# A hybrid GLA and differential-attention layer: a fourth paired projection, branch sums on GpSimd, and an attention whose order of matmuls is a table

## The chip, the cores and the metric

The kernel runs on one core of a Trainium2 chip. The metric is the device time of one execution in microseconds; the time of a kernel is the median of its runs. TensorE is called PE (its weight loads PEld), VectorE DVE, ScalarE ACT, GpSimd POOL; DMAs are issued by SyncE (SP).

## The reference

One layer over 1024 latent tokens x and 256 context tokens, width 1024, all in float32. Cut to what matters here:

```python
pl = project(modulate(x, sh_x, sc_x), w_in)      # 1024 -> 9248 columns, split into:
#  gq 512, gk 512, gv 1024, gate 1024, low rank 32, dq 1024, dk 1024, dv 1024, dgate 1024, m_gla 1024, m_diff 1024
pc = project(modulate(ctx, sh_c, sc_c), w_in)
la = log_sigmoid(lr @ w_dec + b_dec) / 16        # per direction: the decay
o_gla  = bidir_gla(q, k, v, la_f, la_b, s_f, s_b)        # 4 heads, chunks of 64, both directions
a = softmax(q1 k1^T / 8) - lam * softmax(q2 k2^T / 8)    # 8 heads, keys: context + latent = 1280
o_diff = a @ dv
a = merge_heads(rms_norm(o_gla) * gla_gain) * silu(gla_gate)
b = merge_heads(rms_norm(o_diff) * diff_gain * (1 - lam_init)) * silu(diff_gate)
y = sigmoid(m_gla) * (a @ w_br_gla) + sigmoid(m_diff) * (b @ w_br_diff)
out = x + g_x * (y @ w_out)
```

## The kernel before

**Precision.** A float32 operand is split into a rounded part hi and a remainder lo (`split`: a copy on ACT, a subtraction on DVE), and a product is three matmuls (`mm3`: hi hi, hi lo, lo hi) into one PSUM bank. A projection of 1024 inputs onto a tile of 128 x 512 is thus 8 k-blocks x 3 = 24 matmuls.

**The planner.** The program is written as coroutines. `Driver` runs them against a model of the engines' times and so decides, when the kernel is built, in which order instructions stand in each engine's queue. A coroutine waits by yielding an event, a time, or a slot of a tag (`acq`; `rel` gives it back). Lower `prio` goes first. On the chip every engine takes its queue in order. `TAGS` lists the buffers by tag with their pool and count; pools are opened and closed stage by stage.

**Stages.** (1) The prologue: modulation, norm, transposes into `h0`, `h1`, `hc`. (2) `stream` in `phase_a`: projections `gk`, `gq` and the first half of the GLA gate, `gg[0]`, as direct jobs; beside them `job_lr`, `job_la` (the decay), `job_gate` (the ada gate for `w_out`, in `raw` buffers) and `sums` (the block sums s1 to s4 of the layer's input, stored to `d_s`). (3) `pairs`: the projections of `BY7`, which are `gv`, `dv`, `dg`, each by a scheme with seven block products instead of eight. `pair_weights` loads and combines their weights, `loads` brings the sums back into `g5` buffers once `ev_la` and the stored sums are there; `presums` builds, in windows set by `WIN`, the block sums of `w_out`. (4) `to_gla` opens the GLA's buffers; `gla_head` runs four heads in a chain while `stream` goes on with the late jobs as filler: `dk` (two halves), `gg[1]`, `dq` (two halves), and the first half of the mix gates (`post_m`). (5) The attention (`att_scores`, `att_tr`, `att_av`, `att_fin`): for each of 8 heads and 8 query tiles ("score tiles", 64 in all) scores of two components (S), maxima on DVE, exponentials on ACT, the mix of both on DVE, transposes on PE (T), a split into hi and lo (ACT and POOL), and for two query tiles together the product with V (A). `fill` runs beside it with the lowest priority: the rest of the mix gates and the product a @ `w_br_gla`, in half-tiles of 24 matmuls, of which number i is let go when score tile `PACE` x i = 1.3 i has been issued. The planner chooses between S, T, A and fill by priority and readiness. (6) When all scores are done `to_c` opens the last buffers; `prepare` loads the operands of b @ `w_br_diff`, builds their block sums (`OPS`) on DVE and splits them (`SPLITS`); `diff` multiplies seven block products. (7) `right`, `left` and `stream` in `phase_c` do the same for `w_out`, add x and store.

Of the kernel before, what the change touches and what calls it, by code (L numbers as in the profile page):

```python
# [20 lines left out]
P = 128  # L21
# [211 lines left out]
class Hybrid:  # L233
# [18 lines left out]
        ya=("sbC", 8), yb=("sbC", 8), yc=("sbC", 8), yf=("sbC", 8), yg=("sbC", 8), sf=("sbC", 2), o=("sbC", 4), wr=("sbC", 8),  # L252
# [5 lines left out]
                 sbA1="right", sbA2="right", sbW="right", sbB2="right",  # L258
                 psA="left", psW="left", psB="left", psC="left", psA1="right", psB1="right", psD="right")

    def __init__(self, tc, nc, a, out):
        self.tc, self.nc, self.a, self.out = tc, nc, a, out
        self.n = 0
# [17 lines left out]
    def t(self, tag, shape, dt=F32):  # L281
        self.n += 1
        pool, bufs = self.TAGS[tag]
# [92 lines left out]
    def build(self):  # L376
        tc = self.tc
        with (
# [4 lines left out]
            with tc.manual_schedule(engines={ENG.PE, ENG.Activation, ENG.DVE, ENG.Pool}):  # L383
# [8 lines left out]
                self.close("psC", "psW", "psD", "sbW", "sbC", "sb", "sbE")  # L392

    def scratch(self):
# [15 lines left out]
        self.ev_gbt = Event()  # L410
        self.d_y = [d(f"d_y{i}", [P, S]) for i in range(8)]
# [32 lines left out]
    def consts_late(self):  # L444
# [34 lines left out]
        yield from self.rope_tables(1)  # L479
# [271 lines left out]
    def job_gate(self):  # L751
# [5 lines left out]
        for n in range(2):  # L757
            o = 2048 + n * 512
            for kk in range(NK // 2):
                yield from self.acq("raw")  # L760
                raw = self.t("raw", [P, 2, 512])
# [10 lines left out]
                self.rel("raw", e)  # L772
# [22 lines left out]
    def job_tr(self, wd, n, halves, post):  # L795
# [9 lines left out]
        items = [(s, half) for half in halves for s in range(4)]  # L805
# [13 lines left out]
    def phase_a(self):  # L819
# [5 lines left out]
        self.ev_plr, self.ev_lr, self.ev_la, self.ev_gb = [Event() for _ in range(4)]  # L825
# [15 lines left out]
        def tra(c0, halves, post):  # L841
            return c0, lambda wd, n: self.job_tr(wd, n, halves, post)
# [21 lines left out]
        def stream():  # L864
# [4 lines left out]
            for n, j in enumerate(late):  # L869
                if n == 3:  # L870
                    d.spawn(self.rope_tables(0), prio=2)
                yield from j[1](wd2, n)
# [9 lines left out]
        d.spawn(self.job_gate(), At(110.0), prio=2)  # L882
# [11 lines left out]
    BY7 = (("gv", C_GV), ("dv", C_DV), ("dg", C_DG))  # L894

    def sums(self):
# [5 lines left out]
        for k in range(4):  # L902
# [3 lines left out]
            yield from self.acq("g5", 2)  # L906
            x, y = (self.t("g5", [P, 2, 640]) for _ in range(2))
# [1761 lines left out]
```

## Time and profile before

| what | value |
|---|---|
| median of 3 runs | 1625.38 us (1624.56 to 1626.67) |
| the profiled execution's own time | 1624.13 us |
| its span, first to last instruction | 1622.0 us |
| granted PE clock | 1.00 throughout |
| PE instructions | 8277 matmuls |
| HBM | 206.33 MB read, 100.14 MB written |

An engine's busy time is the union of its instructions; the ends of matmuls are modelled, and a matmul of 512 columns is shown as about 389 ns long although the next one starts sooner, so counts in a stretch of time say more of PE's rate than busy times. Lines such as L339 and L201 are helpers through which all matmuls and all ACT, DVE and POOL operations pass; groups are told apart by their tiles, written out<-in.

### The profile page before, as it was taken

Reading aid. Unit: us, or ns where it says so; the run is one execution under the profiler, and the core shown is the slowest. Engines: PE = TensorE matmul, PEld = TensorE weight load, DVE = VectorE, ACT = ScalarE, POOL = GpSimd, SP = SyncE. Lnnn points to the kernel's source line nnn. Section 1 sums busy time; section 2 is a strip of 40 time slices with the busy share of each in tenths; the row PEclk is TensorE's granted clock in tenths of the full one; section 3 lists DMA queues with packets and bytes.
Section 4 is the critical chain, followed back from the end, with each engine's and each line's share of the span. In section 5 each row is a group of like instructions: output and inputs, shape, how many; then the busy total and the mean of one; then the engine's idle time right before and its main releaser. Section 6 shows DMA issues by size and latency. Waiting matters only on the chain.

```text
span 1622.0 us, 24267 instructions
## 1 busy us (share of the span) xinstructions
PE 1601.3 (99%) x8277; PEld 1335.4 (82%) x8277; DVE 1210.8 (75%) x2095; ACT 821.4 (51%) x1689; POOL 596.6 (37%) x647
## 2 busy tenths in 40 slices
PE   8999999999999999999999999999999999999999
PEld 3688888888888888888888788888888888888887
DVE  4788874556678798677772798888888878649994
ACT  4766532244433545564352666666666655535431
POOL 1510200000156566454640446555555556610000
PEclk9999999999999999999999999999999999999999
DMA  8567879688784585655358145443457753354662
GB/s 308 182 214 263 292 241 338 264 309 309 243 271 143 179 256 155 199 156 163 118 163 237 59 124 143 114 121 100 122 134 217 233 143 104 91 191 175 201 220 104
DMA packets 248730, 308.06 MB, mean 190 GB/s; under 512 B 21496, under 2 KB 161696, under 8 KB 248608
## 3 DMA queue, kind: packets, MB, share of 16 engines
q1 hardware_dynamic: 248608, 306.53, 59.7%
q8 instruction: 65, 1.06, 0.3%
q14 instruction: 57, 0.47, 0.1%
HBM read 206.33 MB, written 100.14 MB: 189 GB/s over the span
## 4 chain that ended last, share of the span: by engine, by line
PE 88%; DVE 6%; DMA 2%; ACT 2%; issue 2%; POOL 0%; SPq 0%; DVEq 0%; ACTq 0%
PE mm L339 33%; PE mb L339 10%; PE s L339 8%; PE b L339 7%; PE mc L339 6%; PE tp L339 5%; PE b L365 4%; PE go L339 4%; PE gt L339 4%; PE gs L339 4%; PE tp L365 2%; DVE sm L201 2%; PE mz L339 1%; DVE h L201 1%; ACT e L201 1%
## 5 line engine op out<-in xcount | busy, mean ns | idle before, releaser
L339 PE MATMUL mm<-w,h 128*128 128x512 f32 x1260 | 317.5, 401 | 0.0
L339 PEld LDWEIGHTS mm<-w,h 128*128 128x128 f32 x1260 | 231.6, 188 | 45.9 <-issue 0.5
L201 DVE TENSOR_REDUCE sm<-s 128x1 f32<-128x1024 f32 (+1 forms) x192 | 193.4, 1040 | 43.6 <-PE s L339 41.9
L339 PE MATMUL mb<-h,wt 128*128 128x512 f32 x816 | 220.9, 405 | 1.3 <-DVE ft L201 1.3
L201 ACT ACTIVATE e<-s,sm 128x1280 f32<-128x1280 f32 x128 | 170.1, 1330 | 88.4 <-DVE sm L201 70.3
L201 POOL TENSOR_SCALAR at<-ac 128x512 fp32r<-128x512 f32 x128 | 99.8, 780 | 238.7 <-ACT ac L201 222.9
L339 PE MATMUL s<-hk,aq 128*128 128x512 f32 (+1 forms) x768 | 177.2, 363 | 3.4 <-ACT e L201 2.7
L201 POOL TENSOR_TENSOR at<-ac,at 128x512 fp32r<-128x512 f32 x128 | 174.4, 1363 | 10.7
L339 PEld LDWEIGHTS mb<-h,wt 128*128 128x128 f32 x816 | 144.0, 189 | 26.2 <-DVE ft L201 1.5
L339 PE MATMUL mm<-h,w 128*128 128x512 f32 x576 | 137.8, 394 | 2.0 <-ACT p L201 1.1
L339 PEld LDWEIGHTS s<-hk,aq 128*128 128x128 f32 x768 | 122.1, 189 | 20.9 <-ACT e L201 4.2
L339 PE MATMUL b<-at,vv 128*128 128x256 f32 x960 | 130.8, 287 | 0.0
L339 PEld LDWEIGHTS mm<-h,w 128*128 128x128 f32 x576 | 106.8, 188 | 25.1 <-DVE h L201 1.5
L201 DVE TENSOR_TENSOR w<-raw,w 128x512 fp32r<-128x512 f32 x120 | 87.0, 747 | 47.1 <-ACT w L201 45.8
L339 PEld LDWEIGHTS b<-at,vv 128*128 128x128 f32 x960 | 120.3, 190 | 1.3
L201 POOL TENSOR_TENSOR sm<-sm,nhalf 128x2 f32<-128x2 f32 (+2 forms) x94 | 112.5, 1197 | 20.6 <-DVE sm L201 15.3
L201 DVE SCALAR_TENSOR_TENSOR e<-e,sm,e 128x1280 f32<-128x1280 f32 x64 | 117.7, 1839 | 1.5
L201 ACT ACTIVATE ac<-b 128x512 f32<-128x512 f32 x121 | 72.1, 598 | 83.5 <-PE b L365 83.4
L201 ACT ACTIVATE w<-raw 128x512 fp32r<-128x512 f32 x120 | 72.2, 627 | 72.9 <-PE go L339 21.3
L201 POOL TENSOR_TENSOR p<-p,gdif 128x512 f32<-128x512 f32 x12 | 16.8, 1411 | 238.1 <-DVE p L201 216.0
L201 ACT ACTIVATE p<-mm 128x512 f32<-128x512 f32 (+1 forms) x107 | 61.6, 587 | 76.1 <-PE mm L339 72.5
L365 PE MATMUL b<-ident,e 128*128 128x128 f32 x604 | 93.7, 272 | 0.0
(324 smaller groups left out, 3011.8 us busy)
## 6 DMA issues: line engine op xcount, KB each, us to landing
raw<-in_w_in SPq DMA_DIRECT2D x63, 512.0 KB, 4.7
g<-d_s SPq DMA_DIRECT2D x32, 640.0 KB, 6.1
aq<-d_qT SPq DMA_DIRECT2D x128, 128.0 KB, 3.9
d_dv<-pl SPq DMA_DIRECT2D x40, 256.0 KB, 3.6
gv<-d_v SPq DMA_DIRECT2D x40, 256.0 KB, 3.4
d_kT<-pl SPq DMA_DIRECT2D x40, 256.0 KB, 2.6
hk<-d_kT SPq DMA_DIRECT2D x32, 320.0 KB, 5.1
vv<-d_dv SPq DMA_DIRECT2D x16, 640.0 KB, 6.5
```

The costliest lines, as they stand in the source:

```text
L201: self.ins = f(out, *args, **kw).ins
L339: self.ins = self.nc.tensor.matmul(out, lhsT, rhs, start=start, stop=stop, skip_group_check=more).ins
L365: self.nc.tensor.transpose(out, src, self.ident[:n, :n])
```

## The change

It has these parts.

- The GLA gate becomes a fourth entry of `BY7`; its two direct jobs go. In return the late stream gets half a job more of the mix gates (`NM = 2`, `NS = 2` of 4 column blocks), which `fill` no longer does (`fill_from` 6 in place of 4).
- The stages ahead of the pairs: the decay takes the absolute value on ACT and needs one DVE operation less; `job_gate` starts at 70 in place of 110 and uses `x4`; the reload of the sums waits for new events `ev_lg` and `ev_sg`, set when the last parts hold their `g5` buffers, in place of `ev_la`; the first pair's weights use other buffers; the key's rotary table is loaded later; the four blocks of `presums` go one to each pair.
- Attention: `att_order` writes out one order of all S, T and A; each of them waits for its turn (`turn`, `passed`). Scores run `LEAD = 4` tiles ahead. The first queries are loaded into a `raw` buffer before the GLA has ended.
- `presums_a`: w_br_diff's block sums s1 to s4 are made by POOL during the attention and stored to `d_ps`; `prepare` loads them back. The loads of the last branch's other operands begin once the last scores are done, block by block of the attention's output (`ev_bp`), with buffers that lie in those of keys (`yf`), queries and POOL's inputs (`yg`), and exponentials (`sbD`).

```diff
-        wt=("sbW", 4), ft=("sbW", 2), aq=("sbB2", 4), vv=("sbB2", 3),
-        e5=("sbB", 6), at4=("sbB", 6), at2=("sbB", 2), ac=("sbB", 2), b1k=("sbB", 5), fin=(None, 2),
+        wt=("sbW", 4), ft=("sbW", 2), aq=("sbG", 4), xa=("sbG", 4), vv=("sbB", 3),
+        e5=("sbF", 6), at4=("sbB", 6), at2=("sbB", 2), ac=("sbB", 2), b1k=("sbB", 5), fin=(None, 2),
...
-        jobs = [tra(C_GK, [0, 2, 1], self.post_gk), tra(C_GQ, [0, 1], self.post_gq), gg[0]]
-        late = [dk[0], dk[1], gg[1], dq[0], dq[1]]
-        NM = 1
+        jobs = [tra(C_GK, [0, 2, 1], self.post_gk), tra(C_GQ, [0, 1], self.post_gq)]
+        late = [dk[0], dk[1], dq[0], dq[1]]
+        NM = 2
         for m in range(NM):
-            late.insert(5, tra(C_MG + m * 512, [0, 1], lambda s, half, pm, m=m: self.post_m(4 * m + s, half, pm)))
-        self.fill_from = 4 * NM
+            late.insert(2 + 3 * m, tra(C_MG + m * 512, [0, 1], lambda s, half, pm, m=m: self.post_m(4 * m + s, half, pm),
+                                            self.NS if m else 4))
+        self.fill_from = 4 + self.NS
...
-        d.spawn(self.job_gate(), At(110.0), prio=2)
+        d.spawn(self.job_gate(), At(70.0), prio=2)
...
-    BY7 = (("gv", C_GV), ("dv", C_DV), ("dg", C_DG))
+    NR, NS, TG = 3, 2, 60.0
+    BY7 = (("gv", C_GV), ("dv", C_DV), ("dg", C_DG), ("gg", C_GG))
...
+                    if g == 0:
+                        tag = dict(w111="raw", w211="x4", w120="rope", w221="l5", w121="pl").get(f"{n}{kk}", tag)
...
-    WIN = ((0, 1), (2,), (3,))
+    WIN = ((0,), (1,), (2,), (3,))
...
-            yield self.ev_la
+            yield self.ev_lg
+            yield self.ev_sg
...
-            yield self.act.activation(et, pm, AF.Identity, bias=bcol)
+            yield self.act.activation(et, pm, AF.Abs, bias=bcol)
...
-                    yield self.dve.scalar_tensor_tensor(et, mt, 2.0, et, ALU.mult, ALU.subtract)
...
-                    self.act.activation(ex[j], ex[j], AF.Exp)
+                    self.act.activation(ex[j], ex[j], AF.Exp, scale=-1.0)
...
     def att_queries(self):
-        yield self.ev_b2
+        yield self.wlast
...
+                if (hd, pr) == (0, 0):
+                    yield from self.acq("raw")
+                    early = self.t("raw", [P, 2, 2, 256], F32R)
+                elif (hd, pr) == (0, 1):
+                    yield self.ev_b2
...
     def att_values(self):
-        yield self.ev_q[0, 0]
+        yield self.ev_sb
...
+    LEAD, AHEAD0 = 4, 3
+    def att_order(self):
+        S = lambda u: [("S", u, 0), ("S", u, 1)]
+        T = lambda u: [("T", u, g) for g in range(3)]
+        A = lambda p: [("A", p, 0), ("A", p, 1)]
+        order = sum((S(u) for u in range(self.AHEAD0)), [])
+        for o in range(-1, 65, 2):
+            t, a, s = T(o + 1), A((o - 1) // 2), S(o + self.LEAD + 1)
+            order += T(o) + S(o + self.LEAD) + [t[0], a[0], t[1], a[1], s[0], t[2], s[1]]
+        top = dict(S=64, T=64, A=32)
+        order = [x for n, x in enumerate(order) if 0 <= x[1] < top[x[0]] and x not in order[:n]]
+        self.turns, self.ev_turn = order, {x: Event() for x in order}
+        self.d.set(self.ev_turn[order[0]])
...
+                    yield from self.turn("T", 8 * hd + qt, g)
...
+                    self.passed("T", 8 * hd + qt, g)
...
-    ORDER = ("b11", "b12", "b22", "a12", "b21", "a21", "a22")
+    ORDER = ("b11", "b21", "b22", "a12", "s2", "s1", "s3", "a22", "s4")
...
-        OPS = (("S1", "a21", "a21", "a22", add, ("l_a21", "l_a22"), 2), ("S2", "a11", "a21", "a11", sub, ("S1", "a11"), 2),
-               ("S4", "a12", "a12", "a11", sub, ("S2", "a12"), 4), ("S3", "a11", "a22", "a11", sub, ("S4", "s2"), 4),
-               ("T3", "b12", "b22", "b12", sub, ("l_b12", "l_b22"), 2), ("T2", "b11", "b12", "b11", add, ("T3", "b11"), 2),
+        OPS = (("T3", "b12", "b22", "b12", sub, ("l_b12", "l_b22"), 2), ("T2", "b11", "b12", "b11", add, ("T3", "l_b11"), 2),
...
+    def presums_a(self):
+        d, wb = self.d, self.a["w_br_diff"][0]
+        sub, add = ALU.subtract, ALU.add
+        yield self.ev_sb
+        def op(n, k, o, x, y, f, i):
+            yield self.ev_u[min(63, 2*i+2)]
+            yield d.on("POOL", x, y)
+            self.pool.tensor_tensor(o, x, y, f)
+        for k in range(4):
+            x = {}
+            for r, c in ((1, 0), (1, 1), (0, 0), (0, 1)):
+                yield from self.acq("xa")
+                x[r, c] = self.t("xa", [P, 512])
+                self.dma(x[r, c], wb[c * 512 + k * P:c * 512 + (k + 1) * P, r * 512:(r + 1) * 512])
+            a11, a12, a21, a22 = x[0, 0], x[0, 1], x[1, 0], x[1, 1]
+            ops = (("s1", a21, a21, a22, add), ("s2", a11, a21, a11, sub), ("s4", a12, a12, a11, sub), ("s3", a22, a22, a11, sub))
+            for i, (n, *q) in enumerate(ops):
+                yield from op(n, k, *q, 4 * k + i)
+            for n, o, *_ in ops:
+                self.store([(self.d_ps[n][k], o)], ("xa", 1), ev=self.ev_ps[n, k])
...
-        Z = ("mz", "mz", "mc", "mb")
+        Z = ("mc", "mb", "mz", "mz")
...
+            yield from self.idle("aq", "kk", "xa")
+            Driver.places = tuple(range(512, HK, 512))
+            d.set(self.ev_y0)
+            yield from self.idle("e5")
+            self.close("sbF")
+            self.open("sbD")
+            d.set(self.ev_c1)
             yield self.ev_att
-            yield from self.idle("b1", "e5", "b1k", "aq", "kk", "vv", "at4", "at2", "ac")
-            self.close("psB1", "sbB2", "sbB", "sbK")
+            yield from self.idle("b1", "b1k", "vv", "at4", "at2", "ac")
+            self.close("psB1", "sbB")
```

More of the change, by code (lines that the diff above doesn't have):

```diff
@@ L282, in t @@
         self.n += 1
+        if tag == "yf":
+            self.ny += 1
+            if dt not in self.ys:
+                self.ys[dt] = self.t("hk", [P, HK], dt)
+            x = self.ys[dt][:, (self.ny % 8) * 512:(self.ny % 8 + 1) * 512]
+            self.d.ready[self.d.key(x)] = self.d.now
+            return x
+        if tag == "yg":
+            self.ng += 1
+            tag = ("aq", "xa")[self.ng % 2]
         pool, bufs = self.TAGS[tag]
@@ L804, in post_ @@
             return post(s, half, pm[:, :256 if half == 2 else 512])
-        items = [(s, half) for half in halves for s in range(4)]
+        items = [(s, half) for half in halves for s in range(ns)]
         return self.job(wd, n, items, lambda it, k: [self.ev_h[k, it[1]]],
@@ L977, in free @@
             yield ev_r[g, k]
-            self.rel(slots[g, "w11", k // 2][0], max(e, ev_r[g, k].t), 1 + k // 2)
+            tag = slots[g, "w11", k // 2][0]
+            self.rel(tag, max(e, ev_r[g, k].t), 1 + (tag == "x2"))
         def run():
@@ L2231, in fill @@
             kind = todo[n][0]
-            one = todo[n][:2] in ((1, 6), (1, 7))
+            one = todo[n][:2] in ((1, 6), (1, 7)) or todo[n + 1][0] != kind
             two = [n] if one else [n, n + 1]
@@ L2336, in split @@
             e = yield from self.split(x, *ev[n, k].w)
-            if i > 2 and (src != "a11" or k % 2):
+            if src in ("a11", "e11", "b12"):
+                if k % 2:
+                    self.rel("raw", e)
+            elif i > 2 or src[0] in "as":
                 self.rel(RAW[src], e)
```

151 lines of the change are left out of this document (103 added, 48 removed).

## The prediction

> **What bounds the kernel now.** I read the page's busy times first, then its chain, then the list of what TensorE (PE) waited for.
>
> ```profile
> PE 1601.3 (99%) x8277; PEld 1335.4 (82%) x8277; DVE 1210.8 (75%) x2095; ACT 821.4 (51%) x1689; POOL 596.6 (37%) x647
> ...
> PE 88%; DVE 6%; DMA 2%; ACT 2%; issue 2%; POOL 0%; SPq 0%; DVEq 0%; ACTq 0%
> ```
> ```profile
> engine line waited for: us in total, times, longest us
> PE tp L365 <- DVE p L201: 5.0, 1, 5.0
> PE s L339 <- ACT e L201: 2.7, 3, 1.1
> ```
>
> PE is busy for 1601.3 of 1622.0 us and its longest wait is the 5.0 us before the first transpose, at the start. A busy share can hide gaps between pipelined matmuls, so I cut the span into stages and counted matmuls in them (columns: stretch, length, then busy time and count of PE, PEld, DVE, ACT, POOL, clock, DMA share, GB/s):
>
> ```profile
> 162.00:206.00 44.00, 44.00 (x194) 36.09 (x193) 37.27 (x49) 24.57 (x36) 10.08 (x7) 1.00 0.85 289
> 206.00:302.00 96.00, 96.00 (x426) 79.47 (x425) 57.96 (x88) 29.74 (x51) 3.00 (x2) 1.00 0.87 309
> ...
> 397.50:474.50 77.00, 76.63 (x338) 63.13 (x337) 54.34 (x78) 36.11 (x63) 18.18 (x13) 1.00 0.75 250
> 474.50:887.50 413.00, 412.68 (x2065) 346.40 (x2063) 298.39 (x553) 191.27 (x512) 223.42 (x276) 1.00 0.61 181
> 887.50:1398.00 510.50, 507.25 (x3092) 439.17 (x3093) 424.22 (x784) 317.79 (x642) 283.30 (x264) 1.00 0.47 132
> ```
>
> The first row is the direct job of one half of the GLA gate, the second the paired projection `gv`, the third the paired `dg`, the fourth the GLA beside the late stream, the fifth the attention. In the second row a 512-column matmul costs 96.0/426 = 0.225 us, in the first 44.0/194 = 0.227 us: PE streams without gaps there, at a granted clock of 1.00. So what is taken off PE's count is worth its full price, provided that operands still come in time; and what is only hurried beside PE is worth nothing.
>
> **The gate as a fourth pair.** Before, each half of the gate is 8 tiles x 8 k x 3 = 192 matmuls, and the first half's stage took 44.0 us; the second half costs at least the same in the late stream: 88.0 us together. As a pair it is what `dg` is: 7 products x 4 tiles x 4 k x 3 = 336 matmuls, and that stage took 77.0 us. Saving 88.0 - 77.0 = 11.0 us, on the path. The pair brings the additions on weights and outputs that `dg` has; DVE is at 54.34 of 77.00 us there, so they hide behind PE. If that cover were gone, the stage would last as long as DVE's work: still under 77. Moving one block of presums into each of the four pairs only spreads work that the pairs hide already: 0.
>
> **What must now be ready 44 us earlier.** The first half's direct job stood ahead of the pairs. Without it the first product on the sums s2 comes 44 us sooner:
>
> ```profile
> 234.21 1.98 PE L339 MATMUL mm<-w,g 128*128 128x512 f32 x8
> ```
> ```profile
> 194.03 1.28 SPq L304 DMA_DIRECT2D g<-d_s  x1
> ...
> 205.57 0.32 SPq L304 DMA_DIRECT2D d_s<-g  x1
> ```
> ```profile
> DMA to landing us min/median/max: 2.2/5.2/9.7
> ```
> ```profile
> L201 DVE TENSOR_TENSOR w<-raw,w 128x512 fp32r<-128x512 f32 x120 | 87.0, 747 | 47.1 <-ACT w L201 45.8 <-PE tp L339 0.9 <-PE go L339 0.4
> ...
> L201 DVE SCALAR_TENSOR_TENSOR p<-p,mm 128x512 f32<-128x512 f32 x19 | 12.8, 681 | 1.7 <-ACT p L201 1.5
> ...
> L201 DVE SCALAR_TENSOR_TENSOR g<-g,g 128x1280 f32<-128x1280 f32 x8 | 11.9, 1484 | 0.0
> ```
>
> These are PE's first product on a stored sum, the first reload of a sum and the store of s2's last block, the landing times of these transfers, and DVE groups. The product falls at 234.2 - 44 = 190.2 us; the fourth block of s2 is due 3 x 15 matmuls later, at 190.2 + 45 x 0.225 = 200.3. In this profile that block is stored at 205.6, and with two median transfers of 5.2 us it is back at 216: 16 us late. Against that stands what leaves DVE before it: the eight `g<-g,g` of the decay (11.9 us, which ACT's Abs and the negative scale make needless, at ACT's old cost), the 8 weight splits of the gate's first half (8 x 0.747 = 6.0) and its 8 gate operations (8 x 0.681 = 5.4), 23.3 us in all; the ada gate's sums also start 40 us earlier, in another buffer. DVE is at 37.27 of 44.00 us in this stretch, so most of what leaves it brings the chain forward. The first pair's weights get buffers of their own (`x4`, `rope`, `pl`), so that they don't queue behind `raw`. Bounds 0 and +16 us; I take +1, near the lower end, because 23.3 is more than 16.
>
> **GLA against the late stream.** The late stream loses the gate's second half (44 us) and gains half a job of the mix gate, 4 tiles = 96 matmuls = 22 us, which leaves the attention's fill. On PE's sum that is 0 (bounds -1 and +1). But the stream was what PE did while the GLA's chain ran:
>
> ```profile
> 479.39 0.70 POOL L201 MEMSET fresh<- 128x516 f32 x2
> ```
> ```profile
> 867.49 0.60 PE L365 MATMUL tp<-ident,gp 128*128 128x128 f32 x4
> 867.84 19.34 PE L339 MATMUL mm<-h,w 128*128 128x512 f32 x84
> 887.86 2.60 PE L339 MATMUL s<-hk,aq 128*128 128x512 f32 x12 [0.69 <-ACT p L201]
> ...
> 908.20 1.19 PE L339 MATMUL s<-hk,aq 128*128 128x512 f32 x4 [1.01 <-ACT e L201]
> ...
> 928.62 1.19 PE L339 MATMUL s<-hk,aq 128*128 128x512 f32 x4 [1.09 <-ACT e L201]
> ```
>
> The GLA starts 5 us behind the pairs, and its last transposes end at 868.1, or 393.6 us behind them; the stream ends 413 us behind them, with 19 us of pure stream at the end. Now the stream lasts 413 - 44 + 22 = 391 us. If the GLA keeps its pace, PE runs dry for 393.6 - 391 = 2.6 us: +3. Bounds 0 (the gate's second half also leaves DVE and POOL in this stage) and +8 (the fill's first weights are converted only behind the GLA, where 19 us of stream covered it).
>
> **Entry and tail of the attention.** The first queries are loaded behind the last stream weight into a `raw` slot, not behind the GLA; that holds one of three `raw` slots from the fill's loads until two score tiles are done. The values wait for the closing of the first buffers; they are needed a few tiles later. Three idle times stand at the entry in the fence above (0.69, 1.01, 1.09 us), and one at the tail:
>
> ```profile
> 1405.14 0.96 PE L339 MATMUL mb<-h,wt 128*128 128x512 f32 x3 [1.26 <-DVE ft L201]
> ...
> 1438.46 0.39 PE L365 MATMUL b<-ident,b1k 128*128 128x128 f32 x2
> 1438.60 26.81 PE L339 MATMUL mc<-h,wt 128*128 128x512 f32 x117
> 1465.25 11.04 PE L339 MATMUL mc<-yg,yf 128*128 128x512 f32 x48
> ```
>
> Together they are 4.1 us; I take -3, bounds -4 and +2. From the last score to the last branch's first product the tail is 67 us, and the fill's share of it is in this view of the instructions on its weights, attention and tail:
>
> ```profile
> 887.50:1398.00 510.50, 203.89 (x750) 132.20 (x751) 17.27 (x14) 16.01 (x15) 1.00 0.47 132
> 1398.00:1465.00 67.00, 50.11 (x210) 38.44 (x209) 7.26 (x6) 4.46 (x5) 1.00 0.53 179
> ```
>
> 750 matmuls are 31.25 half-tiles of 24, 210 are 8.75: 40 in all, and 36 after the change. With 31.25 of them in the attention again, 4.75 are left for the tail, 25.7 us in place of 47.3. So the last branch must be able to start 21.6 us earlier, 45 us behind the last score. Its operands a11, b11, a12, b21 are in the buffers of keys, queries and Pool's inputs, which come free at the last score; 16 splits of about 0.75 us are 12 us. The third product needs the last head's last block: its last transposes end at 1438.9 now, the store and the load are two transfers of 5 us, and the first two products (2 x 11 us) stand ahead of it. So 0, and if the cover fails, at most the 21.6 us.
>
> **The order table and Pool's sums.** The four sums of `w_br_diff` leave DVE in the last stage, where PE has no wait, so that gains 0. On Pool they are 16 operations of the kind of its 1.36 us group, 22 us beside 283 of 510 us, and SP issues 32 transfers for them that a DMA share of 0.47 takes.
>
> ```profile
> L201 POOL TENSOR_TENSOR at<-ac,at 128x512 fp32r<-128x512 f32 x128 | 174.4, 1363 | 10.7
> ```
> ```profile
> L201 DVE SCALAR_TENSOR_TENSOR e<-e,sm,e 128x1280 f32<-128x1280 f32 x64 | 117.7, 1839 | 1.5
> ```
>
> DVE's mix of 1280 elements took 1.839 us beside Pool's work, and the same form took 1.484 us in the decay: 0.36 us more. Queued behind each Pool sum are the attention's lo parts, for which A waits; scores run four tiles ahead, so 1.4 us are covered. [...] The table fixes in which order PE takes scores, transposes and products with V. PE's idle time in the attention is the 510.50 - 507.25 = 3.3 us of the row, so a better order can win next to nothing: 0, bounds -3 and the rival below.
>
> **Sum.** -11.0 + 1 + 3 - 3 = -10.0 us. Against the profiled execution's own 1624.13 us (span 1622.0) that is 1614.1; that execution lies 1.25 us under the median 1625.38 of the runs, so the median becomes 1615.4.
>
> **Rivals.** (1) The sums come late: the chain gains only what leaves itself, not the whole 23.3 us. Half of the 16 us remains, +8 in place of +1: 1622.4. For it: DVE at 85%, six `g5` buffers shared by decay, sums and reloads. Against it: 23.3 exceeds 16. Chance 0.14.
>
> (2) Slower: the fill runs out inside the attention. Its pace allows half-tile i from score tile 1.3 i on, so 36 can all be gone at tile 46 of 64; now 31.25 are used over 64. The fixed order makes PE take fill whenever the next entry isn't ready, though another could run. A score tile takes 510.5/64 = 8.0 us; less 750 x 0.225 of fill, PE's own part is 5.3 us, DVE's 424.2/64 = 6.6. Without fill PE idles 1.3 us a tile at DVE's full speed and 2.7 at the present pace, say 2. From 5 such tiles the saving is gone, from 7 the kernel is slower; 12 of the possible 18 give +24: 1639. For it: the fill is smaller and DVE has 6.6 of 8.0 us. Against it: PE took only 0.49 half-tiles a score tile where 0.77 were allowed. Chance 0.10.
>
> (3) All stalls vanish: the GLA gains from the relief of DVE and Pool, entry and sums cost nothing. -11.0 - 4: 1610, down to 1606 if the attention's 3.3 us go as well. Chance 0.12.
>
> The forecast has the rest, 0.64, between 1611 and 1620.
>
> **Numbers.** 0.2%, about what a measurement of this kernel can tell from no change, is 3.3 us: 1622.1 to 1628.6. Faster: forecast 0.64, rival 3's 0.12 and a third of rival 1, 0.05: 0.81. Same: the rest of rival 1, 0.09. Slower: rival 2, 0.10. The range runs from rival 3's end, 1606, to 1627, rival 1 with two thirds of its 16 us and a dry spell of 4 at the GLA's end; rival 2 stays out.
>
> **What would show it.** Right: 48 fewer matmuls of 512 columns (8229 on PE); four pairs from about 162 us, the fourth some 77 us long; the late stream over within 4 us of the GLA's last transposes; fill matmuls left behind the last score; the last branch's first product 45 us behind it. Wrong: PE idle before `mm<-w,g` near 190 us, or `s` waiting for `e` in the attention's last third with no `mb` between.

## The result and the profile after

The changed kernel takes 1631.66 us (median of 6 runs, 1630.03 to 1633.49), the kernel before 1625.85 us beside it: ratio 1.0036, 95% interval 1.0025 to 1.0047. It is slower by 5.8 us; predicted were 10 us less. The profiled execution took 1633.31 us with a span of 1631.6.

The page of the changed kernel, its busy times and chain:

```profile
PE 1599.1 (98%) x8229; PEld 1332.5 (82%) x8229; DVE 1222.1 (75%) x2117; ACT 835.6 (51%) x1719; POOL 633.5 (39%) x663
...
PE 86%; DVE 4%; DMA 3%; issue 3%; POOL 1%; ACT 1%; SPq 1%; POOLq 0%; ACTq 0%; DVEq 0%
```

PE does 48 matmuls less, as forecast, and still ends later. In the profiled execution its span is 9.6 us longer, although 48 matmuls are worth 10.8 us; so PE must stand still, or run slower, by about 20 us more than before. The stages of the changed kernel (columns as in the prediction; the first figure behind POOL's count is the granted clock):

```profile
40.00:80.00 40.00, 36.51 (x182) 27.29 (x180) 29.39 (x46) 28.85 (x55) 20.27 (x31) 0.91 0.65 223
120.00:160.00 40.00, 37.12 (x156) 29.96 (x155) 27.10 (x42) 25.09 (x32) 0.62 (x1) 0.96 0.69 245
171.50:517.50 346.00, 343.87 (x1515) 283.60 (x1514) 228.50 (x336) 144.18 (x241) 45.12 (x31) 1.00 0.82 286
517.50:908.50 391.00, 390.70 (x1970) 328.84 (x1968) 286.52 (x542) 186.99 (x506) 215.32 (x268) 1.00 0.59 175
908.50:1433.00 524.50, 518.61 (x3148) 450.05 (x3149) 436.87 (x799) 318.86 (x645) 320.96 (x285) 1.00 0.55 159
1433.00:1467.80 34.80, 32.90 (x213) 29.40 (x212) 23.75 (x43) 17.47 (x44) 20.36 (x19) 1.00 0.65 207
1467.80:1551.50 83.70, 80.53 (x339) 64.55 (x338) 74.13 (x123) 39.95 (x74) 0.70 (x1) 0.96 0.65 221
```

and three rows of the same view of the kernel before, for the first two stretches and its last branch:

```profile
40.00:80.00 40.00, 36.07 (x199) 27.69 (x198) 29.34 (x48) 28.66 (x56) 20.57 (x36) 1.00 0.58 190
120.00:160.00 40.00, 40.00 (x177) 32.79 (x176) 34.16 (x49) 24.50 (x31) 1.79 (x1) 1.00 0.74 260
...
1465.00:1541.00 76.00, 76.00 (x337) 62.92 (x336) 74.59 (x122) 36.24 (x67) 0.00 (x0) 1.00 0.52 173
```

The four pairs (346.0 us), the GLA's stage (391.0) and the tail behind the last score (34.8) are about what was wanted. But the pairs start at 171.6 and not at 162.0, where the gate's direct job started before: 9.6 us late. And the last branch takes 83.7 us with the matmuls of a 76 us stage. In both places the clock is below 1.00, which it nowhere was in the profiled execution of the kernel before. Cut finer, it is one half in three short stretches (the same view):

```profile
49.80:56.60 6.80, 6.49 (x18) 4.84 (x17) 6.08 (x8) 4.80 (x9) 4.72 (x7) 0.50 0.83 302
1493.60:1500.50 6.90, 6.35 (x13) 4.10 (x14) 5.93 (x11) 6.28 (x13) 0.00 (x0) 0.51 1.03 385
128.30:131.70 3.40, 3.24 (x8) 2.57 (x9) 3.40 (x5) 1.60 (x4) 0.00 (x0) 0.50 0.76 299
```

Half of 6.8 + 6.9 + 3.4 us is 8.5 us lost. Each stretch stands right behind a wait of PE (timeline of the changed kernel, PE; in brackets the idle time and its releaser):

```profile
49.30 1.79 PE L375 MATMUL tp<-ident,g 128*128 128x128 f32 x8 [1.68 <-ACT p L201]
50.74 0.78 PE L349 MATMUL mm<-h,w 128*128 128x512 f32 x1
51.83 10.48 PE L349 MATMUL mm<-h,w 128*128 128x512 f32 x35 [0.31 <-DVE h L201]
...
128.46 6.79 PE L349 MATMUL mm<-h,w 128*128 128x512 f32 x22 [2.88 <-ACT p L201]
...
1484.95 5.71 PE L349 MATMUL mz<-h,wt 128*128 128x512 f32 x24
1492.79 0.73 PE L349 MATMUL mc<-h,h 128*128 128x512 f32 x2 [2.12 <-ACT h L201]
1493.97 14.21 PE L349 MATMUL mc<-h,h 128*128 128x512 f32 x46 [0.45 <-DVE h L201]
```

The 35 matmuls took 10.48 us; before, the same 35 took 8.24 behind a wait of 1.12 us and one of 0.97.

Where the last wait comes from is seen on DVE, SP and ACT (timelines of the changed kernel):

```profile
1480.97 0.69 DVE L201 TENSOR_TENSOR aq<-wr,xa 128x512 fp32r<-128x512 f32 x1 [1.04 <-ACT xa L201]
1481.58 0.42 DVE L201 TENSOR_TENSOR b1k<-b,b1k 128x256 f32<-128x256 f32 x1
...
1484.33 0.48 DVE L201 TENSOR_SCALAR b1k<-b1k,sm 128x128 f32<-128x128 f32 x2 [0.22 <-POOL sm L201]
```
```profile
1466.57 0.37 SPq L314 DMA_DIRECT2D b1k<-d_dg  x1
...
1485.64 0.33 SPq L314 DMA_DIRECT2D d_bT<-b1k  x1
1488.50 0.32 SPq L314 DMA_DIRECT2D yc<-d_bT  x1
1488.88 3.98 SPq L314 DMA_DIRECT2D ya<-d_ps_s  x8
```
```profile
1492.11 0.63 ACT L201 ACTIVATE h<-ya 128x512 fp32r<-128x512 f32 x1 [5.97 <-DMA ya<-d_ps_s]
```

`b1k<-b,b1k` is the finishing step of the attention's very last block. PE had its transposes done at 1465.8, and the block's gate (`b1k<-d_dg`, issued at 1466.6) landed 4.5 us later; from 1471.1 on nothing else was missing. But on DVE the step stood until 1481.6, 10.5 us, behind the last branch's sums (`raw<-yc,raw`, `wr<-raw,wr`, `yc<-yc,wr`) and splits (`h`, `wt`, `aq`). The block is then stored (1485.6) and loaded (1488.5). Only behind that load does SP issue the first reload of Pool's stored sum s2 (`ya<-d_ps_s`, 1488.9), whose buffers `to_c` opens when the attention's last step is done. ACT waits 5.97 us for it and splits it at 1492.1, and PE's third product, which multiplies s2, starts at 1492.8. So what the late block held up first was not its own place in the product but the reload of a Pool sum queued behind it. In the kernel before, this step ran at 1434.5, 31 us ahead of the last branch.

### The profile page after: what moved, and what is told of

It is laid out like the page before. It is cut to its first block, busy times and chain, and to the rows that moved or that the text cites. A ratio compares the mean times of both kernels' runs of the same rounds, so it can differ in the third digit from the quotient of the medians.

```text
span 1631.6 us, 24373 instructions
## 1 busy us (share of the span) xinstructions
PE 1599.1 (98%) x8229; PEld 1332.5 (82%) x8229; DVE 1222.1 (75%) x2117; ACT 835.6 (51%) x1719; POOL 633.5 (39%) x663
## 4 chain that ended last, share of the span: by engine, by line
PE 86%; DVE 4%; DMA 3%; issue 3%; POOL 1%; ACT 1%; SPq 1%; POOLq 0%; ACTq 0%; DVEq 0%
PE mm L349 29%; PE mb L349 10%; PE s L349 7%; PE b L349 6%; PE mc L349 6%; PE tp L349 6%; PE gt L349 5%; PE b L375 4%; PE gs L349 4%; PE go L349 4%; PE mz L349 2%; PE tp L375 2%; SPq L314 1%; DVE sm L201 1%; POOL at L201 1%
## 5 line engine op out<-in xcount | busy, mean ns | idle before, releaser
L349 PE MATMUL mm<-w,h 128*128 128x512 f32 x912 | 231.0, 400 | 0.0
L349 PEld LDWEIGHTS mm<-w,h 128*128 128x128 f32 x912 | 167.4, 188 | 32.7
L201 POOL TENSOR_TENSOR at<-ac,at 128x512 fp32r<-128x512 f32 x128 | 187.9, 1468 | 10.7
L349 PE MATMUL mm<-h,w 128*128 128x512 f32 x672 | 173.2, 407 | 3.2 <-ACT p L201 2.9
L349 PEld LDWEIGHTS mb<-h,wt 128*128 128x128 f32 x840 | 151.1, 188 | 28.3 <-DVE ft L201 0.3
L349 PE MATMUL s<-hk,aq 128*128 128x512 f32 x744 | 168.9, 363 | 2.2 <-ACT e L201 2.0
L349 PEld LDWEIGHTS mm<-h,w 128*128 128x128 f32 x672 | 126.6, 193 | 30.6 <-ACT p L201 3.3
L201 DVE TENSOR_TENSOR w<-raw,w 128x512 fp32r<-128x512 f32 x128 | 96.1, 768 | 53.8 <-ACT w L201 52.7
L349 PE MATMUL mm<-w,g 128*128 128x512 f32 x432 | 105.7, 389 | 0.0
L349 PEld LDWEIGHTS mm<-w,g 128*128 128x128 f32 x432 | 81.1, 188 | 16.8
```

What stands on the lines that cost most here:

```text
L201: self.ins = f(out, *args, **kw).ins
L349: self.ins = self.nc.tensor.matmul(out, lhsT, rhs, start=start, stop=stop, skip_group_check=more).ins
```

## The experiments

In the table "clock" is the mean granted clock of a kernel's runs and "at full clock" the mean of each run's span times its clock, which takes the half-clock time out where PE sets the pace. The clock has three decimals, so a single value is good to about 0.8 us; the kernel before, run beside each set of versions (107 executions in all), gave means from 1621.5 to 1622.4 from one set to the next. Times and ratios are good to what the intervals say: where two overlap, the versions are not told apart by them.

| kernel | median us | ratio to before, 95% interval | clock | at full clock |
|---|---|---|---|---|
| before | 1625.85 | | 0.9988 | 1621.9 |
| changed | 1631.66 | 1.0036 (1.0025 to 1.0047) | 0.9952 | 1622.3 |
| stages before the attention alone | 1647.78 | 1.0136 (1.0122 to 1.0150) | 0.9915 | 1632.3 |
| attention and last branch alone | 1630.24 | 1.0025 (1.0016 to 1.0035) | 0.9988 | 1626.5 |
| without the order table | 1655.30 | 1.0179 (1.0165 to 1.0193) | 0.9942 | 1643.7 |
| finishing steps raised | 1627.12 | 1.0006 (0.9997 to 1.0015) | 0.9970 | 1620.3 |
| the same, without Pool's arithmetic | 1628.04 | 1.0009 (0.9999 to 1.0018) | 0.9964 | 1619.6 |
| ada gate at 110 | 1629.21 | 1.0023 (1.0014 to 1.0032) | 0.9967 | 1622.5 |
| steps raised, ada gate at 110 | 1626.68 | 1.0005 (0.9996 to 1.0014) | 0.9974 | 1620.5 |
| the same through `raw` | 1626.48 | 1.0004 (0.9995 to 1.0013) | 0.9975 | 1620.8 |
| splits' rank lowered | 1624.20 | 0.9995 (0.9986 to 1.0004) | 0.9973 | 1618.6 |
| splits' rank lowered, ada gate at 110 | 1623.31 | 0.9985 (0.9976 to 0.9994) | 0.9986 | 1619.3 |
| before with three waits of 3 us | 1645.44 | 1.0118 (1.0102 to 1.0133) | 0.9943 | 1634.1 |

**The two halves of the change.** The kernel before, with the first three stages' edits alone (the gate as a pair, `NM`, `NS`, decay, `job_gate`, sums), then with the others alone (order table, early queries, `presums_a`, `prepare`, buffers).

> The kernel before with only the first half of the change: the gate as fourth pair and all that is done ahead of and in the pairs, with the old attention and last branch. Theory (two places lose what the gate saves, and a half clock on PE doubles the loss of each): -11.0 for the gate, +3 in the prologue, +5 between 83 us and the pairs, 0 elsewhere, so 3 us under before (ratio 0.998). Rival (the first half keeps its 11 us whole, all the loss is in the attention and behind it): 11 us under before (0.993).

> The kernel before with only the second half of the change: order table, Pool's sums, early loads of the last branch. The gate stays two direct jobs and the fill has its 40 half-tiles. Theory (the last head's finishing steps queue on DVE behind the splits of the last branch, and PE then goes to half clock): +4 in the attention and +7 at the third product of the last branch, 11 us over before (1.007), less if the four more half-tiles of fill cover it. Rival (only the smaller fill costs): 0, within 2 us of before.

The first half alone is much worse than foreseen, 22 us over the kernel before where 3 or 11 under it were expected. Its pairs start at 172.1 us, so the late start belongs to this half. With 4 half-tiles of fill less, the old loads of the attention and the last branch lie open (the longest of PE's waits behind 900 us; total, times, longest):

```profile
PE mc L339 <- DVE yg L201: 5.3, 6, 2.1
PE s L339 <- DMA aq<-d_qT: 4.8, 1, 4.8
PE mc L339 <- ACT yc L201: 2.8, 2, 1.6
```

The second half alone costs 4.1 us at full clock (1626.5 against 1622.4 of the kernel before beside it), with waits of up to 1.3 us spread over the attention; neither expectation held. Its last branch has none: its tail behind the last score is 55.6 us long, in place of the 34.8 of both halves together. So the last branch's wait comes only from both.

**The order table.** `turn` and `passed` do nothing, else as changed.

```diff
-        yield self.ev_turn[x]
+        return
+        yield
```

> The changed kernel without the order table: scores, transposes and products with V go by priority and readiness as before. Theory (the table costs the attention some 4 us and uses 34 half-tiles of fill in place of 31): 2 to 5 us less than the changed kernel, with 4 to 5 half-tiles left behind the last score. Rival (the table is what makes the kernel slower): 10 us less, at or under before.

23.6 us slower than the changed kernel, where both expectations had it faster: with these buffers and early loads the table is needed. It isn't where the loss comes from.

**The last blocks' finishing steps.**

```diff
-   ... On(e, "ACT"), prio=self.PF)
+   ... On(e, "ACT"), prio=-4 if (hd, pr) >= (7, 2) else self.PF)
```

> The changed kernel with one thing altered: the finishing coroutine of the last head's last two pairs has priority -4 in place of -2, so that the planner puts its DVE steps ahead of the splits of the last branch. Theory: the last block of the attention's output is stored some 10 us sooner, PE's 3 us of waiting before the third product of the last branch go and with them the half clock of 6.8 us: 6 to 7 us less than the changed kernel (ratio to before 0.9995). Rival (the tail is short of cover because the fill is used up): under 2 us less.

4.5 us come back, 2.0 of them at full clock; the expectation was 6 to 7. In the profile the wait ahead of the third product is gone, but waits of 0.44, 0.23 and 1.08 us stand inside that product. With the raised steps the prediction's Pool term could be tried by itself:

```diff
-            self.pool.tensor_tensor(o, x, y, f)
```

> The version with the finishing steps raised (1627.1 us), and Pool's 16 additions and subtractions for the sums of `w_br_diff` left out: their loads and stores stay, so the stored sums are not sums. It prices Pool's arithmetic in the attention. The prediction put it at 0; if so, 1626 to 1628 us and the attention from first to last score stays at 524 us. [...]

The times of the two agree within their spread. Without Pool's arithmetic the attention's stretch, first to last score, lasts 523.4 us, with DVE busy for 436.23 and POOL for 294.02; in the changed kernel, whose rank of the last steps is the old one, it lasts 524.5, with 436.87 and 320.96. DVE's mix took 1.839 us on the mean in the kernel before and 1.861 in the changed one. So Pool's 16 operations cost at most about 1.1 us here, and nothing that shows in the time: the term 0 stands.

**The ada gate's loads.** In the changed kernel they stand ahead of two of the first projection's weights on SP (41.55 against 44.36 us), and ACT, which splits those weights, waits 0.82 us for them where it waited 0.25; PE's transposes are behind that in ACT's queue.

```diff
-        d.spawn(self.job_gate(), At(70.0), prio=2)
+        d.spawn(self.job_gate(), At(110.0), prio=2)
```

> The changed kernel with one number put back: the ada gate's sums start at 110 us by the planner's clock instead of 70, so their first loads no longer stand on SP's queue ahead of the weights for the first projection. Theory: these loads delay `w<-raw` on ACT near 47 us, PE waits 1.7 us, and 6.8 us at half clock follow. Then PE's wait near 47 us falls to about 1.1 us, the half-clock stretch at 49.8 us is gone, the first projection starts near 80 us instead of 83.5, and the kernel takes about 1627 to 1629 us (3 to 4 us less than the changed one's 1631.7; 2 us more if the stretch near 128 us goes too). Rival: the half-clock stretches fall by chance of the moment and have nothing to do with these loads; then the time stays within 1 us of 1631.7.

> The changed kernel with both edits: the last blocks' finishing steps raised ahead of the last branch's operand splits (which alone gave 1627.1 us), and the ada gate's sums started at 110 us again. If the two losses are independent of each other, as the theory has them, the gains add: about 1623 us, 1620 if the wait near 125 us goes too. Rival: a half-clock stretch taken away at one place comes back at another, since PE still waits somewhere in each part; then the time stays at 1626 to 1628.

> As the kernel with both edits, but the ada gate's loads also go through the buffers `raw`, as before the change, and not `x4`: they then queue for buffers with the weights and come much later. Theory: what hurt was where the loads stand on SP's queue, so this gives the same 1620 to 1623 us as the other, with no half clock before 200 us. Rival: the loads in `raw` hold up the weights of the first pair; then the first product on the sums comes later than in the changed kernel and the time is 1627 or more.

Put back, they bring 2.5 us, with overlapping intervals; the mean clock is 0.9967 where it was 0.9952. At full clock nothing changes (1622.5 and 1622.3), so whatever was won is clock. That the loads cause the half clock is not shown: in the profile of the version through `raw`, which has the gate at 110 too, the eight transposes at 48.0 us and the matmul behind them take 1.78 and 0.78 us, as at the changed kernel's half clock near 50 us (1.79 and 0.78), where the kernel before took 1.32 and 0.47. On top of the raised steps the late start brings 0.4 us only, within the spread: the gains did not add as the theory said, and PE ran slow elsewhere: behind a wait of 1.91 us twelve matmuls of A take 2.52 us at 1442.8 us, where the same twelve, behind the same wait, take 1.67 in the changed kernel.

**What a wait of PE costs.** The kernel before, with a chain of small ACT operations ahead of a zero matmul in each pair's t2 product (7 operations) and t1 product (1):

```diff
+                        if (k, t) == (2, 0):
+                            self.act.activation(self.z2, A[nt - 1][:, :256], AF.Copy, scale=0.0)
+                            for _ in range(6 if n == "p6" else 0):
+                                self.act.activation(self.z2, self.z2.bitcast(F32), AF.Copy, scale=0.0)
+                            self.mm(A[0][:, :256], self.zz, self.z2, False, False, True)
```

> The kernel BEFORE with six waits put into the paired products, where PE otherwise streams without a gap: in each of the three pairs a chain of 7 small ACT operations (about 3 us) ahead of one matmul with zero weights in t2's product, and a single such operation (0.5 to 1 us) in t1's. It measures what a wait of PE costs by itself. Rival, and what the prediction assumed: a wait costs its length, 3 x 3 + 3 x 1 = 12 us, 1638 us, and the granted clock stays at 1.00. Theory: behind each long wait PE runs 3.4 or 6.8 us at half clock, and each of these costs 1.7 to 3.4 us more: 1643 to 1648 us, with stretches of clock 0.5 right behind the three long waits and none behind the short ones.

> As the earlier kernel with six waits in the paired products of the kernel BEFORE, but the chain of small ACT operations now starts from the last matmul issued, so that nothing covers it: three waits of about 3 us (7 operations) and three of about 1 us (1 operation). Rival, the prediction's assumption: a wait costs its length, 12 us together, 1638 us, clock 1.00. Theory: a wait of 3 us is followed by 3.4 or 6.8 us at half clock in part of the executions, a wait of 1 us in the middle of a full stream is not: 1640 to 1646 us, the mean clock falls to 0.994 to 0.998, and the stretches lie behind the long waits only.

In the first version the chain began at an earlier matmul (`A[0]`) and was mostly hidden: 1629.50 us, 1.0024 (1.0015 to 1.0032), 5.3 us over the kernel before at full clock (1626.8 against 1621.5), with mean clocks from 0.998 to 1.000 in its eleven executions. In the second version the three waits are real (timeline of PE):

```profile
245.79 0.39 PE L339 MATMUL mm<-z,zz 128*128 128x256 f32 x1 [3.16 <-ACT z L201]
246.03 2.24 PE L339 MATMUL mm<-w,g 128*128 128x512 f32 x9
...
345.55 0.39 PE L339 MATMUL mm<-z,zz 128*128 128x256 f32 x1 [3.16 <-ACT z L201]
345.77 3.09 PE L339 MATMUL mm<-w,g 128*128 128x512 f32 x9
...
440.20 0.58 PE L339 MATMUL mm<-z,zz 128*128 128x256 f32 x1 [3.16 <-ACT z L201]
440.58 4.05 PE L339 MATMUL mm<-w,g 128*128 128x512 f32 x9
```

Three equal waits, three prices: behind the first, nine matmuls take their usual 2.24 us, at a clock of 1.00 (246 to 260 us); behind the second 3.09, with a mean clock of 0.91 from 342 to 360 us, which is 3.2 us at one half; behind the third 4.05, with 0.74 from 437 to 450 us, which is 6.8 us at one half. The waits, six with the three short ones, cost 11.8 us at full clock (1634.1 - 1622.3 of the kernel before beside it) and 18.9 in time. So they cost 1.6 times their length on the mean of four executions, whose clocks lie between 0.993 and 0.997: the draw differs from one to the next.

In the changed kernel's profile such stretches stand behind waits of other lengths: 6.8 us at 0.50 behind 1.68 us in the prologue, with smaller waits beside it, 3.4 us at 0.50 behind 2.88 us near 125 us, and 6.9 us at 0.51 behind 2.12 us in the last branch. What decides how much half clock follows a wait, no run here shows.

**Filling the waits.** Matmuls with zero weights in PE's order, at the changed kernel's wait near 1490 us (nine of 512 columns, as below); near 47 and 125 us (14 and 24 of 128 columns); both of these with the steps raised; and two versions whose idle matmuls are left out of the planner's model, at all three places and, with the steps raised, at the first two.

```diff
+                    if (n, t, k) == (1, 3, 3):
+                        for _ in range(9):
+                            e = self.mm(A[3], self.zz, rh, False, False, True)
```

> The changed kernel with nine idle matmuls (512 columns, zero weights, 2.0 us) put into PE's order just ahead of the product of the last branch for which PE waited 2.3 us at 1490 us: they add zero, and nothing else is moved. Theory: the half-clock stretch of 6.8 us behind that wait comes from PE standing still. Then the stretch near 1494 us is gone, about 3.4 us are saved at no cost, and the time is 1628 to 1629 us against 1631.7. Rival: the clock falls for another reason (its moment, the load of other engines); then the stretch stays and the time stays within 1 us of 1631.7, or rises by up to 2 us for the added matmuls.

> The same test at the two other waits of the changed kernel: 14 idle matmuls of 128 columns (about 1.4 us) in the wait near 47 us and 24 (about 2.4 us) in the one near 125 us. Theory: the stretches of 6.8 and 3.4 us behind them are gone and 3.4 + 1.7 us are saved: 1626 to 1628 us. [...] Rival: no effect of filling the waits, 1631 to 1634.

> The idle matmuls of the first 130 us together with the raised finishing steps of the last attention blocks (alone 1627.1 us). Theory: little half clock is left anywhere, and what the change saves on PE shows at last: 1621 to 1624 us, under the 1625.8 of the kernel before. Rival: half-clock stretches come back at the other waits (25 us, 938 us, 1443 us), as they did when the ada gate's loads were put back: 1626 to 1628.

> The changed kernel with idle matmuls of zero weights in its three waits (16 of 128 columns near 47 us, 26 near 125 us, nine of 512 columns near 1490 us), hidden from the planner, so that the order of all else stays. Theory: they turn standing still into work of no use and take away the half clock alone. At full clock the changed kernel's spans come to 1622 us, as before's do: 1624 to 1627 us in place of 1631.7, mean clock 0.998 or more. Rival: the half clock does not hang on these waits, 1630 to 1633.

> The finishing steps of the last attention blocks raised (alone 1627.1 us), and idle matmuls hidden from the planner in the waits near 47 us (20) and 125 us (26). Theory: the clock loss of about 5 us that is left in the kernel with raised steps (mean clock 0.997) falls to 1 or 2 us: 1622 to 1625 us, under before's 1625.8. Rival: the half clock comes back at other waits or stays: 1626 to 1629.

| kernel | median us | ratio to before, 95% interval | clock | at full clock |
|---|---|---|---|---|
| near 1490 us | 1629.66 | 1.0025 (1.0016 to 1.0034) | 0.9968 | 1622.8 |
| near 47 and 125 us | 1641.91 | 1.0099 (1.0086 to 1.0112) | 0.9955 | 1632.8 |
| the same, steps raised | 1639.84 | 1.0082 (1.0069 to 1.0095) | 0.9962 | 1631.3 |
| all three, left out of the model | 1632.76 | 1.0039 (1.0027 to 1.0052) | 0.9980 | 1628.2 |
| 47 and 125 us, left out of the model, steps raised | 1636.16 | 1.0054 (1.0041 to 1.0066) | 0.9956 | 1626.7 |

With the wait near 1490 us filled, the profiled execution has a mean clock of 0.999: at most 2.4 us are lost to it in all, and a stretch of 6.9 us at one half costs 3.4. But in that execution the wait of 1.41 us near 47 us, which is not filled, has no half clock behind it either (the 35 matmuls there take 8.27 us, 8.24 in the kernel before), so a single one proves little. The median is 2.0 us lower and the mean clock 0.0016 higher, but the intervals overlap and the twelve executions range from 1626.3 to 1632.8 us. In the front it fails. In the profile with all three no half clock follows the idle matmuls near 47 and 125 us (the 35 matmuls behind the first take 8.23 us, the 21 behind the second 5.00, where 22 took 6.79), but near 125 us PE now comes later, and they are plain work:

```profile
127.46 3.01 PE L773 MATMUL tp<-zz 128*128 128x128 f32 x26
```

This is the kernel with all three. SP's order shifted in a few places too, ACT waited 5.50 us for `g<-in_x` where it had waited 1.53, and PE ran slow behind new waits at 63 us: 15 matmuls take 5.25 us there, 3.66 in the changed kernel. Its mean clock is 0.998 as foreseen; the work it added took the gain away.

**The splits' rank.** If the last branch's operations on DVE are what holds up the attention's last steps, lowering them is the cure for both late waits:

```diff
-                    d.spawn(split(n, k, *SPLITS[n]), prio=-3 + 0.1 * SPLITS[n][2])
+                    d.spawn(split(n, k, *SPLITS[n]), prio=-1.9 + 0.1 * SPLITS[n][2])
...
-                d.spawn(op(k, *x), prio=-3.05 + 0.1 * x[-1])
+                d.spawn(op(k, *x), prio=-1.95 + 0.1 * x[-1])
```

> The changed kernel with the rank of the last branch's operand splits and sums lowered by 1.1, below the attention's own mixes, parts and finishing steps; their loads stay as early. Theory: the same queueing on DVE makes both late waits. Then PE's wait of 1.9 to 2.1 us before the last product with V near 1443 us shrinks to about 1 us (two of the four splits go behind it), the wait near 1490 us shrinks as it did with the raised finishing steps, and the time is 1625 to 1627 us against 1631.7 (1627.1 with the raised steps alone). Rival: the last branch's first operands now come later and its first product waits; then a new wait of 2 us or more near 1465 us and 1628 to 1632 us.

> The same with the ada gate's sums started at 110 us again. Theory: fewer waits of over 1.5 us leave less half clock: 1622 to 1626 us, level with or under before's 1625.8. Rival: the clock falls behind the remaining waits as often as before, 1626 to 1629.

The wait before the third product is gone (timeline of PE, ranks lowered):

```profile
1481.17 5.60 PE L349 MATMUL mz<-h,wt 128*128 128x512 f32 x24
1486.61 11.04 PE L349 MATMUL mc<-h,h 128*128 128x512 f32 x48
```

and so is the one near 1443 us; one of 1.1 us on `b1k` is left there. The last block's step runs on DVE at 1465.4, as soon as its gate has landed, and SP issues the reload of s2 at 1473.7. 7.5 us come back, 3.7 of them at full clock. With the ada gate at 110 as well it is 1623.31 us, ratio 0.9985 (0.9976 to 0.9994): the only version that beats the kernel before, by 2.5 us where 10 were forecast. The stage in it (compare 83.70 above):

```profile
1464.80:1541.70 76.90, 76.72 (x339) 63.21 (x338) 71.98 (x120) 39.04 (x73) 1.68 (x1) 1.00 0.68 233
```

## Why the prediction was wrong

In the two profiled executions the span grew by 9.6 us. The parts are: the start of the pairs +9.6 (forecast 0), the pairs and the GLA +11.1 (forecast 15.0 with the sums and the GLA's dry spell), from the first score to the last branch -18.1 (forecast -24.6), the last branch +7.7 (forecast 0), the rest -0.9.

**The gate as a fourth pair: right.** The pairs and the GLA's stage together, from the gate's old start or the pairs' new one to the first score, grew by 11.1 us (736.9 against 725.8), which is 77 - 44 for the fourth pair less 22 for the late stream, to the half microsecond.

**The stored sums: in time, but by luck.** PE is busy without a gap from the start of the pairs through the first product on a sum at 198.8 us, so the term +1 was 0. The last block of s2, though, had little to spare (SP and PE of the changed kernel):

```profile
200.41 0.61 SPq L314 DMA_DIRECT2D g<-d_s  x1
```
```profile
208.98 2.20 PE L349 MATMUL mm<-w,g 128*128 128x512 f32 x9
```

The load landed 6.7 us after its issue, at 207.1, 1.9 us ahead of its product. The prediction had this product due at 200.3; it came at 209.0 because the pairs started 9.6 us late. The store of the block moved from 205.6 to 196.2, 9.4 us sooner where the argument "23.3 is more than 16" needed about 16. Had the pairs started at 162.0 with the sums where they are, PE would have waited some 7 us here, which is what rival 1 describes. How far the sums would then have come sooner too was not tried.

**GLA against the late stream: +3 was too much.** PE is busy for 390.70 of 391.00 us; the first score waits 0.25 us. The prediction let the GLA keep its pace; its last transposes end 390.7 us behind the pairs instead of 393.6, just as the stream ends.

**The start of the pairs: not priced.** They came 9.6 us late. Of `job_gate`'s earlier start the prediction wrote only that the ada gate's sums start 40 us earlier in another buffer, as a help to DVE. It did not say which loads stand behind its loads on SP. In the profiled execution 5.1 of the 9.6 us are half clock (half of 6.8 + 3.4), 2.9 the wait near 125 us, 1.0 other waits of PE and 0.5 five matmuls more ahead of the pairs. The ada gate's start explains only part: with the old one back, the pairs start at 165.6, waits of 1.52 us at 121.6 and 1.68 us at 171.2 stand in place of the one near 125, and at full clock nothing is won. What makes the wait near 125 us stays open. On ACT the decay's four operations follow each other from 121.8 to 127.9 ahead of PE's evictions, and just before them ACT waits 2.65 us for a weight's load (`raw<-in_w_in`); neither was tried by itself.

**Entry and tail waits: -3 became about +3.5.** From the first score to the last branch's first product it took 559.3 us (577.4 before): 18.1 saved, where 24.6 were counted (21.6 of fill and 3 of waits). The waits of the changed kernel, of which the lines on `b1k`, `e` and `at` lie here:

```profile
PE mm L349 <- ACT p L201: 2.9, 1, 2.9
PE b L375 <- DVE b1k L201: 2.8, 5, 1.3
PE tp L375 <- ACT p L201: 2.7, 2, 1.7
PE mc L349 <- ACT h L201: 2.1, 1, 2.1
...
PE s L349 <- ACT e L201: 2.0, 2, 1.8
PE b L349 <- DVE at L201: 1.9, 1, 1.9
```

Rival 2 named the fixed order, and the second half alone shows such waits; but fill did not run out (72 of its matmuls, three half-tiles, were left for the tail), and the mechanism as it was priced did not happen.

**"So 0, and if the cover fails at most 21.6 us": the step that failed most.** The prediction asked whether the last branch's operands come early enough, and they do: its first product comes 35 us behind the last score, even earlier than the 45 forecast. It priced the last block's way to the third product as a store and a load behind transposes that end as early as before. It did not ask who is queued behind the 16 splits of 0.75 us and the sums on DVE, which now run while the attention's last steps are due, and at a rank ahead of them. The last block's finishing step was such a one and stood there for 10.5 us: its last transposes came 51.7 us behind the last score (1484.7 against 1433.0), where they had come 40.5 us behind it. Nor did it see that the reloads of Pool's sums, which it priced at 0, stand behind this block on SP and feed the same product. The stage took 7.7 us more, 3.4 of them half clock. Lowering the rank alone gave 7.5 us back, more than the whole loss against the kernel before.

**Waits at their length: the wrong price throughout.** The sum took 1.00 for the clock and each wait at its own length. The changed kernel at full clock equals the kernel before (1622.3 and 1621.9); the loss of 5.8 us in the medians is the clock's, 0.9952 against 0.9988. So the failure has two layers: waits of some 11 us ate the 11 us that were saved on PE, and behind them the half clock took another 6. Of the 15.8 us between forecast and result, the lowered rank brings back 7.5 and the ada gate's old start 0.9 more, within the spread; the rest lies in the start of the pairs and in the attention, and its cause is open.

**Moved fill, Pool's sums: right at 0.** The order table was more than 0: it is worth 23.6 us among the other edits, while the half of the change that it belongs to costs 4.1 us by itself.

## What to carry to other kernels

When loads and splits are moved forward, ask of each engine's queue what now stands behind them, with its rank, and who needs that last; an operand that is early by 10 us can delay the one that is due. Where PE streams without gaps, price a new wait of 3 us at about one and a half times its length (18.9 us for 11.8 here, from one kernel), and compare kernels by their granted clock as well as by their time. Two halves of a change that are each harmless at a place can make a wait there together, so the cover of a step has to be counted in the kernel that has both.

## What was not expected of the hardware

Waits of PE of 1.7 to 3.2 us, in the changed kernel, where PE is busy for 98% of the span, and in the kernel before with three waits put in, were followed by 3.2 to 6.9 us at half clock, in some executions and not in others: eleven runs of the kernel with raised steps lie between 1622.7 us, at a mean clock of 0.999, and 1630.4 us, at 0.994. Waits of 1.26 and 1.09 us in the kernel before, near 1404 and 928 us, were not followed by it (1.00 behind both). Nor was every longer one: behind the first of the three equal waits of 3.16 us the clock stayed at 1.00.
